# Attention of a two-layer encoder by pairs of heads: scores on the two halves of the array's rows, values on the two halves of its columns

## The chip, the cores and the metric

One core of one Trainium2 chip runs the kernel. The metric is the device time of one execution in microseconds (us), the median of the runs shown. The engines are TensorE (PE, with its weight loads PEld), VectorE (DVE), ScalarE (ACT), GpSimd (POOL) and SyncE (SP, which issues DMAs). Each engine works through its own instructions in a fixed order and waits at an instruction until what it needs is there.

## The reference

Two layers, 512 tokens, 1024 channels. Cut to what the change touches:

```
proj = h @ w_in[layer]                       # 2048 columns: pool | q | k | v
y_pool = pool_mixer(u_pool, ...)             # 4 groups of 128, trailing means over 2, 4, 8, 16
# stick-breaking attention, 8 heads of 64:
z = einsum('bhtd,bhsd->bhts', qb, kb) * scale
log_1m_beta = where(mask, log_sigmoid(-z), 0)
between = cumsum(log_1m_beta, axis=3, reverse=True) - log_1m_beta
att = where(mask, exp(log_sigmoid(z) + between), 0)
y_sb = einsum('bhts,bhsd->bhtd', att, vb)
mix = concat([y_pool, y_sb]) @ w_out[layer]
h = LayerNorm(alpha * h + mix);  h = LayerNorm(alpha * h + FFN(h))   # dense, then top-2-of-8 experts
```

## The kernel before

Numbers are kept as pairs of float16 (a high part and a rest), so each product is three matmuls: high by high, high by rest, rest by high. Each layer begins with a mixer, the part that the change touches; the dense layer and the experts after it are the same before and after.

In the mixer all is laid out with the source position on the partitions. A head's scores z stand in three banks of PSUM (pool `pz`, two tiles), 1280 columns: four blocks of 512, 384, 256 and 128 columns, since only later positions look at a block. `head_z` (L326) makes them from q and k: a head has 64 channels, so its 12 matmuls use 64 of the array's 128 rows, the lower half for an even head and the upper half for an odd one. Then, in two parts of 768 and 512 columns, ACT forms abs, exp and ln (L330 to L332), DVE adds max(z, 0) (L333), POOL masks the diagonal blocks (L344), and DVE splits the result into two float16 tiles (L346, L347). `head_att` adds the reverse running sum to z by matmuls with a triangle and with ones (L355, L360; 20 matmuls), ACT takes exp (L364), and POOL and DVE mask and split again. `head_out` (L379) multiplies by v: 12 matmuls on all 128 columns of the array for the 128 channels of a pair of heads, of which ACT copies the head's own 64 partitions into `cat` (L381).

The loop over heads issues, for each head `hd`: `head_att(hd)`, `head_out(hd - 1)`, one or two `pool_map`s if there are any, `head_z(hd + 2)`, and then a piece of other work of about 10 us on PE: the projection of a later pair's q and k (`qk_proj`), two groups of the pooling mixer (`pool`), v's second half (`v_proj`), the split of `cat`, or the output projection (`w_out`). `pool` makes u by 48 matmuls; `pool_group` copies it (ACT L284), forms the trailing sums on DVE (L290 to L298) and splits them (ACT L274 into `pdh`, DVE L276 into `pdl`); `pool_map` is three matmuls (L310 to L312) and a copy by ACT (L313). A scheduler puts the instructions of the whole program into one order per engine when the kernel is built; in the mixer that order follows the order in which the code issues the work, with small moves.

Three stores matter. `pa` has two PSUM tiles (tag `acc`), taken in turns by `qk_ps`, `u_ps`, `v_ps`, `o_ps`, `pool_ps` and `mix_ps`: a new one waits until the one before the last has been copied out. `pz` has two tiles, one for each of two heads. The weights of the mixer are split long before they are used (ACT L153, DVE L154); the rows of L153 and L154 that stand between the heads belong to the output projection.

Of the kernel before, what the change touches and what calls it, by code (L numbers as in the profile page):

```python
# [17 lines left out]
P = 128  # L18
D = 1024
# [44 lines left out]
class Trunk:  # L64
# [248 lines left out]
        nc.scalar.activation(cat[:, g, :], ps, AF.Copy, scale=sc[:, g:g + 1])  # L313


    def head_z(self, hd, qk):
        nc, mm = self.nc, self.nc.tensor.matmul
        (qh, ql), (kh, kl) = qk
        r = slice(hd % 2 * HD, (hd % 2 + 1) * HD)
        z = self.pz.tile([P, 1536], F32, tag="z", name="z")  # L320
        for i in (1, 3, 2, 0):
            T = S - i * P
            o = z[:, ZOFF[i]:ZOFF[i] + T]
            ks = slice(i * P, (i + 1) * P)
            for n, (kk, qq) in enumerate(((kh, qh), (kl, qh), (kh, ql))):
                mm(o, kk[r, ks], qq[r, i * P:], start=(n == 0 and i != 3), stop=False, skip_group_check=True)  # L326
        t = self.bp.tile([P, W], F32, tag="bf", name="t", bufs=3)
        s2 = self.head_pair()
        for c, blocks in HALVES:
            nc.scalar.activation(t[:, c], z[:, c], AF.Abs)  # L330
            nc.scalar.activation(t[:, c], t[:, c], AF.Exp, scale=-1.0)
            nc.scalar.activation(t[:, c], t[:, c], AF.Ln, bias=1.0)  # L332
            nc.vector.scalar_tensor_tensor(t[:, c], z[:, c], 0.0, t[:, c], op0=ALU.max, op1=ALU.add)  # L333
            self.head_two(t, s2, c, blocks)
        return z, t, s2

    def head_pair(self):
        return [self.bp.tile([P, W], F16, tag="br", name="sh", bufs=4) for _ in range(2)]

    def head_two(self, t, s2, c, blocks, scale=1.0):  # L340
        nc = self.nc
# [23 lines left out]
            self.head_two(t, a2, c, blocks, AS)  # L365
        return a2

    def head_out(self, hd, a2, v, cat):
        nc, mm = self.nc, self.nc.tensor.matmul
        vh, vl = v  # L370
        ah, al = a2
        p = hd // 2
        r = slice(hd % 2 * HD, (hd % 2 + 1) * HD)
        o = self.pa.tile([P, 512], F32, tag="acc", name="o_ps")
        c = slice(p % 2 * P, (p % 2 + 1) * P)
        for i in (1, 2, 3, 0):
            T = S - i * P
            for n, (vv, x) in enumerate(((vh, ah), (vh, al), (vl, ah))):
                mm(o[:, i * P:], vv[:, i, c], x[:, ZOFF[i]:ZOFF[i] + T], start=(i == 1 and n == 0),  # L379
                   stop=(i == 0 and n == 2), skip_group_check=True)  # L380
        nc.scalar.activation(cat[r, 4 + p, :], o[r, :], AF.Copy, scale=1.0 / (AS * VS))  # L381


    def mixer(self, l, h, hs, first=None):
# [24 lines left out]
        def qk_proj(p, ps=None):  # L409

            w = self.unit(win[2 + p])
            acc = [self.pa.tile([P, 512], F32, tag="acc", name="qk_ps") if ps is None else ps[:, 512 * s:512 * s + 512]
                   for s in range(2)]
            qk[p] = [tuple(mp.tile([P, S], F16, tag=f"qk{s}", name="qk", bufs=4) for _ in range(2)) for s in range(2)]
            for ts in (slice(0, S),) if ps is None else (slice(0, S // 2), slice(S // 2, S)):
                for s, sc in ((0, QS * XS), (1, KS * XS)):
                    self.chan_major(acc[s][:, ts], hs, w, s, ts)
                    if ts.stop == S:
                        self.two(*qk[p][s], acc[s], sc)
                    yield  # L420
# [18 lines left out]
        if first:  # L439
            with tc.issue_after(self.normed[1]), tc.issue_after(self.normed[2]):  # L440
                self.constants(self.cp, mp.tile([P, 16 + S], F32, tag="pf", name="room", bufs=2))
        zt, at = {}, {}
        zt[0] = self.head_z(0, qk[0])
        zt[1] = self.head_z(1, qk[0])
        list(qk_proj(1))
        ms = None
        wu = {}
# [19 lines left out]
        def cat_split(ks):  # L467
            for k in ks:
                self.two(ms[0][:, k], ms[1][:, k], cat[:, k, :].rearrange("p (t c) -> p t c", c=P))

        early = (4, 5, 0, 1, 2, 3)
        for hd in range(2 * NPAIR - 1):
            at[hd] = self.head_att(zt.pop(hd))
            if hd >= 1:
                self.head_out(hd - 1, at.pop(hd - 1), v, cat)
            for n in range(1 + (hd > 3)):
                if maps:
                    g, d2 = maps.pop(0)
                    self.pool_map(params, g, d2, cat)
            if hd + 2 < 2 * NPAIR:  # L480
                zt[hd + 2] = self.head_z(hd + 2, qk[(hd + 2) // 2])
            if hd == 0:
                list(qk_proj(2))
            elif hd == 1:
                pool(0)
            elif hd == 2:
                pool(1)
            elif hd == 3:
                list(qk_proj(3))
            elif hd == 4:  # L490
                list(v_proj(1))
                ms = self.act_tiles(self.hp, "k t")
                cat_split(early)
            elif hd == 5:
                for tt in range(NT):
                    w_out(0, early, tt)
        at[7] = self.head_att(zt.pop(7))
        cat_split((6,))
        for tt in range(NT):
            w_out(1, (*early, 6), tt)  # L500
        for hd in (6, 7):
            self.head_out(hd, at.pop(hd), v, cat)
        cat_split((7,))
        wu[2] = self.unit(a["w_out"][l, 2])
        ctx.close()
# [738 lines left out]
    def build(self, dump=None):  # L1244
        nc, tc, a = self.nc, self.tc, self.a
        with ExitStack() as ctx:
            self.ctx = ctx
            pool = lambda name, bufs, **k: ctx.enter_context(tc.tile_pool(name=name, bufs=bufs, **k))
            cp = self.cp = pool("const", 1)
            self.sp = pool("small", 2)  # L1250
            self.rps, self.n_raw, self.ahead = [pool("raw", RAW)], 0, []
            self.wp = pool("split", 6)
            self.chain, self.feed, self.fed, self.pending = None, None, False, []
            hpool = pool("h", 1)
            self.pa = pool("pa", 2, space=PSUM)
            dram = pool("dram", 1, space=DRAM)
            self.H = dram.tile([S, D], F32, name="H")
            self.H2 = dram.tile([S, D], F32, name="H2")
            self.Y = dram.tile([NOROW + 1, D], F32, name="Y")
            self.hctx = ExitStack()  # L1260
            self.hp = self.hctx.enter_context(tc.tile_pool(name="act", bufs=1))
            self.ident = cp.tile([P, P], F32, name="ident")
            make_identity(nc, self.ident)
            self.mhalf = cp.tile([P, 1], F32, name="mhalf")
            nc.vector.memset(self.mhalf, -0.5)
            h = hpool.tile([P, NT, D], F32, name="h")
            nc.sync.dma_start(h[:, 0, :], a["x"][0:P, :])
            hs = self.act_tiles(self.hp)
            self.todo = {}

            def first(mp):
                gt, bt = (mp.tile([P, W], F32, tag="bf", name=n, bufs=3)[:, :D] for n in ("gt", "bt"))
                keep = tc.keep_in_program_order
                keep(nc.sync.dma_start(gt, a["ln_in_g"].to_broadcast([P, D])))
                keep(nc.sync.dma_start(bt, a["ln_in_b"].to_broadcast([P, D])))

                def norm(tt):
                    if tt > 0:
                        keep(nc.sync.dma_start(h[:, tt, :], a["x"][tt * P:(tt + 1) * P, :]))
                    self.ln_tile(h[:, tt, :], h[:, tt, :], gt, bt)  # L1280

                def step(pool, tt):
                    if tt + 1 < NT:
                        norm(tt + 1)
                    self.transpose_tile(hs, h[:, tt, :], tt, pool)

                norm(0)
                self.todo = {tt: lambda pool, tt=tt: step(pool, tt) for tt in range(NT)}

            def show():  # L1290
                for tt in range(NT):
                    nc.sync.dma_start(a["out"][tt * P:(tt + 1) * P, :], h[:, tt, :])
                self.a2ctx.close()
                self.hctx.close()

            for l in range(DEPTH):
                hs = self.mixer(l, h, hs, None if l else first)
                if dump == f"mix{l}":
                    return show()
                if l == 0:  # L1300
                    hs = self.dense(h, hs, a["ln2_g"][l:l + 1], a["ln2_b"][l:l + 1])
                    if dump == "ffn0":
                        return show()
                    self.a2ctx.close()
                else:
                    self.moe(h, hs, a["out"], a["ln2_g"][l:l + 1], a["ln2_b"][l:l + 1])
# [56 lines left out]
```

## Time and profile before

| | |
|---|---|
| median of 3 runs | 1627.39 us (1625.93 to 1628.72) |
| profiled execution | 1625.76 us, its span 1624.0 us |
| PE busy | 94% of the span |
| DVE, ACT, POOL busy | 73%, 57%, 11% |
| mean granted clock of PE | 0.986 of 2.4 GHz |
| first layer's mixer, heads | about 50 to 180 us |
| second layer's mixer, heads | about 588 to 717 us |

A matmul's duration in the trace holds its way through the array, so that durations of matmuls that follow each other overlap; what one costs PE is read from start to start. The same holds, less so, on DVE and ACT: an instruction starts some 0.1 us before the one ahead ends if it doesn't need its result.

### The profile page before, as it was taken

The page shows a single profiled execution, that of the slowest core. Times are in us where ns is not written, and L with a number is a line of the kernel's source. Part 1 is how long each engine was busy: PE and PEld are TensorE (multiplying, and loading weights), DVE is VectorE, ACT ScalarE, POOL GpSimd, SP SyncE. Part 2 cuts the span into 40 slices and gives each one's busy share as a digit, 9 for nine tenths or more (in the row PEclk, how much of TensorE's full clock was granted, in tenths as well). Part 3 has the DMA queues.
Part 4 walks back from the last instruction along what each step waited for, and adds up shares of the span by engine and source line. Part 5 has one row for each costly group of instructions (what it writes and reads, how often), then busy time and mean ns, then how long its engine had stood idle before and what let it go on. Part 6 is the DMA issues. An engine that isn't in the chain of part 4 may idle for free.

```text
span 1624.0 us, 41584 instructions
## 1 busy us (share of the span) xinstructions
PE 1530.3 (94%) x17978; PEld 1277.5 (79%) x17978; DVE 1184.5 (73%) x1682; ACT 929.8 (57%) x1276; POOL 178.1 (11%) x297
## 2 busy tenths in 40 slices
PE   6999999999999999998999999995999999999975
PEld 4547774674755865686999999995999999999975
DVE  8786673333433767758998988876788799898986
ACT  5656243222223355624587877764677678777861
POOL 4122110000000212212000001000000000000423
PEclk9999999999999999999999999997999999999997
DMA  8410153222322132024899999898699869999992
GB/s 301 173 53 27 53 207 104 98 78 101 110 89 94 62 130 78 27 103 158 319 344 388 377 383 360 308 338 284 231 383 335 317 243 418 414 393 356 340 367 88
DMA packets 61840, 366.75 MB, mean 226 GB/s; under 512 B 9654, under 2 KB 13582, under 8 KB 28628
## 3 DMA queue, kind: packets, MB, share of 16 engines
q1 hardware_dynamic: 55044, 351.65, 58.1%
q0 software_dynamic: 5312, 9.21, 2.4%
q10 hardware_dynamic: 1296, 3.18, 0.6%
q8 instruction: 142, 2.33, 0.6%
q14 instruction: 46, 0.38, 0.1%
HBM read 353.17 MB, written 10.84 MB: 224 GB/s over the span
## 4 chain that ended last, share of the span: by engine, by line
PE 51%; issue 26%; DVE 7%; DMA 6%; ACT 3%; POOL 3%; POOLq 0%; SPq 0%; ACTq 0%; DVEq 0%
PE gu L1158 24%; PE acc L1158 14%; DVE wl L154 3%; DMA xr<-H,idx 3%; PE z L326 1%; DMA raw<-in_moe_wd 1%; PE qk_ps L267 1%; PE qk_ps L268 1%; PE qk_ps L269 1%; POOL rs L220 1%; ACT wh L153 1%; DMA h<-Y,r_rows 1%; PE yt_ps L1213 1%; DMA H<-h 1%; PE z L360 1%
## 5 line engine op out<-in xcount | busy, mean ns | idle before, releaser
L154 DVE SCALAR_TENSOR_TENSOR wl<-raw,wh 128x512 f16<-128x512 f32 (+2 forms) x506 | 754.3, 1516 | 59.0 <-ACT wh L153 55.7
L153 ACT ACTIVATE wh<-raw 128x512 f16<-128x512 f32 (+2 forms) x506 | 631.1, 1274 | 264.3 <-PE gu L268 90.5
L1158 PEld LDWEIGHTS <-wh 128*128 128x128 f16 x8448 | 668.0, 97 | 3.1 <-DVE xT L1153 2.3
L1158 PE MATMUL gu<-xT,wh 128*128 128x128 f16 (+6 forms) x5632 | 522.9, 224 | 2.2 <-DVE xT L1153 2.2
L1158 PE MATMUL gu<-xT,wl 128*128 128x128 f16 (+6 forms) x2816 | 517.8, 223 | 0.0
L1158 PEld LDWEIGHTS <-wl 128*128 128x128 f16 x4224 | 416.6, 99 | 3.2 <-issue 3.1
L1158 PE MATMUL acc<-hT,wh 128*128 128x128 f16 (+6 forms) x2816 | 261.9, 225 | 3.1 <-DVE hT L1180 2.9
L1158 PE MATMUL acc<-hT,wl 128*128 128x128 f16 (+6 forms) x1408 | 259.4, 223 | 0.0
L268 PE MATMUL gu<-hTl,wh 128*128 128x512 f16 (+1 forms) x384 | 138.7, 361 | 0.5 <-DVE hTl L276 0.5
L267 PE MATMUL gu<-hTh,wh 128*128 128x512 f16 (+1 forms) x384 | 138.7, 361 | 0.0
L269 PE MATMUL gu<-hTh,wl 128*128 128x512 f16 (+1 forms) x384 | 138.7, 361 | 0.0
L588 DVE SCALAR_TENSOR_TENSOR sg<-gu,sg 128x512 f32<-128x512 f32 (+1 forms) x24 | 15.5, 646 | 138.7 <-PE gu L269 138.7
L267 PEld LDWEIGHTS <-wh 128*128 128x128 f16 x608 | 59.5, 98 | 61.6 <-issue 3.1
L269 PEld LDWEIGHTS <-wl 128*128 128x128 f16 x608 | 59.5, 98 | 59.2 <-issue 1.3
L268 PEld LDWEIGHTS <-wh 128*128 128x128 f16 x608 | 59.5, 98 | 58.3 <-issue 2.5
L1175 ACT ACTIVATE sg<-gu 128x128 f32<-128x128 f32 (+6 forms) x176 | 49.7, 283 | 89.1 <-PE gu L1158 85.7
L611 PE MATMUL d_ps<-wh,tl 128*128 128x256 f16 x352 | 96.0, 273 | 0.1
L611 PE MATMUL d_ps<-wh,th 128*128 128x256 f16 x352 | 95.9, 273 | 0.0
L611 PE MATMUL d_ps<-wl,th 128*128 128x256 f16 x352 | 95.9, 273 | 0.0
L1128 POOL DMA_INDIRECT xr<-H,idx x12 | 22.6, 1883 | 627.3 <-DMA raw<-in_moe_gu 399.5
L344 POOL TENSOR_SCALAR_AFFINE_SELECT t<-t 128x128 f32<-128x128 f32 x128 | 58.7, 486 | 185.9 <-DVE t L333 131.8
L1179 ACT ACTIVATE hT<-hu 128x128 f16<-128x128 f32 (+6 forms) x176 | 55.5, 315 | 36.3 <-DVE hu L1177 33.9
(226 smaller groups left out, 1933.7 us busy)
## 6 DMA issues: line engine op xcount, KB each, us to landing
raw<-in_moe_gu SPq DMA_DIRECT2D x176, 1024.0 KB
raw<-in_moe_wd SPq DMA_DIRECT2D x64, 896.0 KB
raw<-in_moe_wd SPq DMA_DIRECT2D x32, 1024.0 KB
raw<-in_ffn_gu SPq DMA_DIRECT2D x22, 1024.0 KB
raw<-in_w_in SPq DMA_DIRECT2D x16, 1024.0 KB
raw<-in_w_out SPq DMA_DIRECT2D x8, 1024.0 KB
raw<-in_ffn_wd SPq DMA_DIRECT2D x8, 896.0 KB
raw<-in_ffn_wd SPq DMA_DIRECT2D x4, 1024.0 KB
```

The costliest lines, as they stand in the source:

```text
L153: self.link(lambda: self.nc.scalar.activation(wh[:, c], raw[:, c], AF.Copy, scale=WS))
L154: self.link(lambda: self.nc.vector.scalar_tensor_tensor(wl[:, c], raw[:, c], WS, wh[:, c], op0=ALU.mult, op1=ALU.subtract))
L220: nc.gpsimd.tensor_tensor(rs, ve, self.mhalf, op=ALU.pow)
L267: mm(ps, wh[:, k, :], hh[:, k, ts], start=(k == 0), stop=False)
L268: mm(ps, wh[:, k, :], hl[:, k, ts], start=False, stop=False)
L269: mm(ps, wl[:, k, :], hh[:, k, ts], start=False, stop=(k == KD - 1))
L344: nc.gpsimd.affine_select(out=b, in_=b, pattern=[[1, P]], base=0, channel_multiplier=-1, compare_op=ALU.is_gt, fill=0.0)
L611: nc.tensor.matmul(ps[:, :256], hid[f][x][:, ts], v[:, f - f0, :], start=(f == f0 and n == 0), stop=(f == f1 - 1 and n == 2))
L1128: nc.gpsimd.indirect_dma_start(out=xr[b], out_offset=None, in_=self.H, in_offset=bass.IndirectOffsetOnAxis(ap=idx[b], axis=0), bounds_chec ...
L1158: self.nc.tensor.matmul(o, w, x[:, a], start=(start and n == 0), stop=(stop and n == 2), skip_group_check=True)
L1175: self.link(lambda: nc.scalar.activation(sg, ps[:, :N], AF.Silu, scale=XS))
L1179: self.link(lambda: nc.scalar.activation(hT[:, 0, :], hu, AF.Copy))
```

## The change

`head_z` becomes `pair_z`: both heads of a pair, with their matmuls in turns (even head, odd head), each on its half of the rows. `head_out` becomes `pair_out`: each head multiplies by its own 64 columns of v, in turns, into its own 64 partitions of one `o_ps`, and one copy by ACT (L385) takes all 128 partitions. The loop goes over pairs: attention of both heads, then the other work, then the next pair's scores, this pair's values, and behind them the pool maps and the next projection. Buffers: `t` 4 for 3, the split tiles 6 for 4.

```
-    def head_z(self, hd, qk):
+    def pair_z(self, qk):
...
             for n, (kk, qq) in enumerate(((kh, qh), (kl, qh), (kh, ql))):
-                mm(o, kk[r, ks], qq[r, i * P:], start=(n == 0 and i != 3), stop=False, skip_group_check=True)
+                for s, z in enumerate(zs):
+                    r = slice(s * HD, (s + 1) * HD)
+                    mm(z[:, ZOFF[i]:ZOFF[i] + T], kk[r, ks], qq[r, i * P:], start=(n == 0 and i != 3), stop=False,
+                       skip_group_check=True)
...
-    def head_out(self, hd, a2, v, cat):
+    def pair_out(self, p, a2s, v, cat):
...
-                mm(o[:, i * P:], vv[:, i, c], x[:, ZOFF[i]:ZOFF[i] + T], start=(i == 1 and n == 0),
-                   stop=(i == 0 and n == 2), skip_group_check=True)
-        nc.scalar.activation(cat[r, 4 + p, :], o[r, :], AF.Copy, scale=1.0 / (AS * VS))
+                for s, a2 in enumerate(a2s):
+                    c = slice(p % 2 * P + s * HD, p % 2 * P + (s + 1) * HD)
+                    mm(o[s * HD:(s + 1) * HD, i * P:], vv[:, i, c], a2[a][:, ZOFF[i]:ZOFF[i] + T],
+                       start=(i == 1 and n == 0), stop=(i == 0 and n == 2), skip_group_check=True)
+        nc.scalar.activation(cat[:, 4 + p, :], o, AF.Copy, scale=1.0 / (AS * VS))
...
+        for p in range(NPAIR):
+            at = [self.head_att(x) for x in zt]
+            if p < 2:
+                pool(p)
+            elif p == 2:
+                pool_maps()
+                list(v_proj(1))
+            else:
+                cat_split((6,))
+                for tt in range(NT):
+                    w_out(1, (*early, 6), tt)
+            if p + 1 < NPAIR:
+                zt = self.pair_z(qk[p + 1])
+            self.pair_out(p, at, v, cat)
+            if p < 2:
+                pool_maps()
+                list(qk_proj(2 + p))
+            elif p == 2:
+                ms = self.act_tiles(self.hp, "k t")
+                cat_split(early)
                 for tt in range(NT):
                     w_out(0, early, tt)
```

On PE, behind the first half of the pooling mixer in the first layer, before: the values of head 1, one pool map, then the scores of head 4 (z_1047).

```order
L379 MATMUL o_ps_1028<-sh_847,vl_196 128x512
L310 LDWEIGHTS pw_h_468
L310 MATMUL pool_ps_1042<-pdh_951,pw_h_468 128x512
L311 LDWEIGHTS pw_h_468
L311 MATMUL pool_ps_1042<-pdl_952,pw_h_468 128x512
L312 LDWEIGHTS pw_l_469
L312 MATMUL pool_ps_1042<-pdh_951,pw_l_469 128x512
L326 LDWEIGHTS qk_773
L326 MATMUL z_1047<-qk_771,qk_773 128x384
```

On PE at the same place in the changed kernel: the last values of the pair (sh_713 is head 0's, sh_745 head 1's), both pool maps (pool_ps_938, pool_ps_943), and the next projection.

```order
L383 MATMUL o_ps_912<-sh_713,vl_196 64x512
L383 LDWEIGHTS vl_196
L383 MATMUL o_ps_912<-sh_745,vl_196 64x512
L310 LDWEIGHTS pw_h_468
L310 MATMUL pool_ps_938<-pdh_803,pw_h_468 128x512
...
L310 LDWEIGHTS pw_h_468
L310 MATMUL pool_ps_943<-pdh_844,pw_h_468 128x512
...
L267 LDWEIGHTS wh_950
L267 MATMUL qk_ps_960<-hTh_90,wh_950 128x512
```

Two `pool_ps` and a `qk_ps` now follow `o_ps` directly, all in the two tiles of `pa`; before, one map stood there and the scores, which have tiles of their own, came next.

On ACT, from the copy of the second group's u onward, before: the copy of `o_ps` (L381) stands two rows ahead of the first part of the next head's abs (L330), and `pdh` of the second group behind that.

```order
L284 ACTIVATE cat_119<-u_ps_955 128x512
L153 ACTIVATE wh_1945<-raw_1943 128x512 x3
L364 ACTIVATE t_738<-z_725 128x768
L364 ACTIVATE t_738<-z_725 128x512
L381 ACTIVATE cat_119<-o_ps_1028 64x512
L313 ACTIVATE cat_119<-pool_ps_1042,pw_s_472 128x512
L330 ACTIVATE t_1060<-z_1047 128x768
L274 ACTIVATE pdh_992<-pd_988 128x512
```

On ACT at the same place in the changed kernel (t_874 and t_893 are the two heads of the next pair, pdh_844 the second group's).

```order
L284 ACTIVATE cat_119<-u_ps_807 128x512
L153 ACTIVATE wh_1805<-raw_1803 128x512 x3
L334 ACTIVATE t_874<-z_848 128x768
L334 ACTIVATE t_893<-z_849 128x768
L335 ACTIVATE t_874<-t_874 128x768
L274 ACTIVATE pdh_844<-pd_840 128x512
L336 ACTIVATE t_874<-t_874 128x768
L335 ACTIVATE t_893<-t_893 128x768
L385 ACTIVATE cat_119<-o_ps_912 128x512
L334 ACTIVATE t_874<-z_848 128x512
L336 ACTIVATE t_893<-t_893 128x768
L335 ACTIVATE t_874<-t_874 128x512
```

The copy of `o_ps` has moved behind the `pdh` of the second group and behind five rows of the next pair; the copy of the first map (L313) is the row after the last one shown.

## Rows read from the trace of the kernel before

**Rows 1.** The page, busy time, share of the span and instructions of each engine.

```profile
PE 1530.3 (94%) x17978; PEld 1277.5 (79%) x17978; DVE 1184.5 (73%) x1682; ACT 929.8 (57%) x1276; POOL 178.1 (11%) x297
```

**Rows 2.** Windows in both mixers: stretch, length, busy time (instructions) by engine, granted clock, DMA.

```profile
61.00:97.00 36.00, 34.51 (x205) 18.16 (x205) 27.19 (x49) 23.45 (x39) 8.19 (x22) 1.00 0.16 59
97.00:134.00 37.00, 36.14 (x208) 18.35 (x206) 29.74 (x55) 23.13 (x38) 12.36 (x27) 1.00 0.17 57
...
636.00:672.00 36.00, 35.60 (x205) 18.19 (x205) 29.15 (x54) 22.67 (x38) 11.44 (x25) 1.00 0.18 59
```

**Rows 3.** Timeline of PE, rows with idle time: start, us, instructions, [idle before <-releaser].

```profile
61.42 0.49 PE L355 MATMUL z<-sh,ntri 128*128 128x128 f16 x4 [0.46 <-DVE t L333]
...
63.96 0.38 PE L355 MATMUL z<-sh,ntri 128*128 128x512 f16 x1 [1.07 <-DVE sh L347]
...
115.18 1.79 PE L326 MATMUL z<-qk 64*128 64x384 f16 x12 [0.86 <-ACT t L364]
...
149.73 1.79 PE L326 MATMUL z<-qk 64*128 64x384 f16 x12 [0.30 <-ACT t L364]
```

**Rows 4.** Timeline of PE around the scores of one head.

```profile
66.12 0.38 PE L267 MATMUL qk_ps<-hTh,wh 128*128 128x512 f16 x1
66.44 1.80 PE L326 MATMUL z<-qk 64*128 64x384 f16 x12
68.17 0.39 PE L268 MATMUL qk_ps<-hTl,wh 128*128 128x512 f16 x1
```

**Rows 5.** Timeline of PE at heads 0 and 1, whose scores follow each other.

```profile
51.63 2.53 PE L326 MATMUL z<-qk 64*128 64x384 f16 x23
54.09 0.39 PE L269 MATMUL qk_ps<-hTh,wl 128*128 128x512 f16 x1
```

**Rows 6.** Timeline of PEld in 52.2 to 52.6, the same place.

```profile
52.13 0.49 PEld L326 LDWEIGHTS <-qk 64*128 64x128 f16 x7
```

**Rows 7.** Timeline of PE from a head's values to the pool map behind them.

```profile
95.22 0.49 PE L379 MATMUL o_ps<-sh,vh 128*128 128x384 f16 x2
...
96.85 0.38 PE L310 MATMUL pool_ps<-pdh,pw_h 128*128 128x512 f16 x1
97.07 0.38 PE L311 MATMUL pool_ps<-pdl,pw_h 128*128 128x512 f16 x1
```

**Rows 8.** Timeline of ACT after the last matmul of a pooling half.

```profile
93.02 0.63 ACT L153 ACTIVATE wh<-raw 128x512 f16<-128x512 f32 x1 [1.35 <-PE u_ps L268]
93.56 0.58 ACT L284 ACTIVATE cat<-u_ps 128x512 f32<-128x512 f32 x1
94.04 1.65 ACT L153 ACTIVATE wh<-raw 128x512 f16<-128x512 f32 x3
```

**Rows 9.** Timeline of DVE right behind it.

```profile
94.30 0.15 DVE L290 COPY ps<-cat 128x1 f32<-128x1 f32 x1
...
94.96 0.68 DVE L154 SCALAR_TENSOR_TENSOR wl<-raw,wh 128x512 f16<-128x512 f32 x1
95.56 0.68 DVE L293 TENSOR_TENSOR ps<-ps 128x512 f32<-128x512 f32 x1
```

**Rows 10.** Groups of ACT by shape in 48 to 215: count | busy us, mean ns | idle before.

```profile
L331 ACT ACTIVATE t<-t 128x768 f32<-128x768 f32 x8 | 6.7, 840 | 0.2
...
L381 ACT ACTIVATE cat<-o_ps 64x512 f32<-64x512 f32 x8 | 4.7, 590 | 12.0 <-PE o_ps L379 12.0
...
L313 ACT ACTIVATE cat<-pool_ps,pw_s 128x512 f32<-128x512 f32 x4 | 2.7, 685 | 0.5 <-PE pool_ps L312 0.3
L274 ACT ACTIVATE pdh<-pd 128x512 f16<-128x512 f32 x4 | 2.5, 629 | 8.2 <-DVE pd L298 8.2
```

**Rows 11.** Timeline of PE in the experts, behind its idle time at 792 to 795.

```profile
794.90 0.19 PE L1042 MATMUL sl_ps<-terms,hot 128*128 128x6 bf16 x2 [3.05 <-DVE terms L1027]
```

**Rows 12.** Windows of PE alone: stretch, length, busy (instructions), granted clock, DMA.

```profile
796.20:799.50 3.30, 3.30 (x38) 0.50 0.99 353
1139.00:1144.30 5.30, 5.30 (x49) 0.50 0.01 3
```

More of the change, by code (lines that the diff above doesn't have):

```diff
@@ L313, in pool_map @@
         nc.scalar.activation(cat[:, g, :], ps, AF.Copy, scale=sc[:, g:g + 1])
-    def head_z(self, hd, qk):
+    def pair_z(self, qk):
         nc, mm = self.nc, self.nc.tensor.matmul
         (qh, ql), (kh, kl) = qk
-        r = slice(hd % 2 * HD, (hd % 2 + 1) * HD)
-        z = self.pz.tile([P, 1536], F32, tag="z", name="z")
+        zs = [self.pz.tile([P, 1536], F32, tag="z", name="z") for _ in range(2)]
         for i in (1, 3, 2, 0):
             T = S - i * P
-            o = z[:, ZOFF[i]:ZOFF[i] + T]
             ks = slice(i * P, (i + 1) * P)
             for n, (kk, qq) in enumerate(((kh, qh), (kl, qh), (kh, ql))):
-                mm(o, kk[r, ks], qq[r, i * P:], start=(n == 0 and i != 3), stop=False, skip_group_check=True)
[L327 to L335, printed above, removed]
+                for s, z in enumerate(zs):
+                    r = slice(s * HD, (s + 1) * HD)
+                    mm(z[:, ZOFF[i]:ZOFF[i] + T], kk[r, ks], qq[r, i * P:], start=(n == 0 and i != 3), stop=False,
+                       skip_group_check=True)
+        pair = []
+        for z in zs:
+            t = self.bp.tile([P, W], F32, tag="bf", name="t", bufs=4)
+            s2 = self.head_pair()
+            for c, blocks in HALVES:
+                nc.scalar.activation(t[:, c], z[:, c], AF.Abs)
+                nc.scalar.activation(t[:, c], t[:, c], AF.Exp, scale=-1.0)
+                nc.scalar.activation(t[:, c], t[:, c], AF.Ln, bias=1.0)
+                nc.vector.scalar_tensor_tensor(t[:, c], z[:, c], 0.0, t[:, c], op0=ALU.max, op1=ALU.add)
+                self.head_two(t, s2, c, blocks)
+            pair.append((z, t, s2))
+        return pair
     def head_pair(self):
-        return [self.bp.tile([P, W], F16, tag="br", name="sh", bufs=4) for _ in range(2)]
+        return [self.bp.tile([P, W], F16, tag="br", name="sh", bufs=6) for _ in range(2)]
     def head_two(self, t, s2, c, blocks, scale=1.0):
@@ L366, in head_att @@
         return a2
-    def head_out(self, hd, a2, v, cat):
+    def pair_out(self, p, a2s, v, cat):
         nc, mm = self.nc, self.nc.tensor.matmul
         vh, vl = v
-        ah, al = a2
-        p = hd // 2
-        r = slice(hd % 2 * HD, (hd % 2 + 1) * HD)
         o = self.pa.tile([P, 512], F32, tag="acc", name="o_ps")
-        c = slice(p % 2 * P, (p % 2 + 1) * P)
         for i in (1, 2, 3, 0):
             T = S - i * P
-            for n, (vv, x) in enumerate(((vh, ah), (vh, al), (vl, ah))):
-                mm(o[:, i * P:], vv[:, i, c], x[:, ZOFF[i]:ZOFF[i] + T], start=(i == 1 and n == 0),
-                   stop=(i == 0 and n == 2), skip_group_check=True)
-        nc.scalar.activation(cat[r, 4 + p, :], o[r, :], AF.Copy, scale=1.0 / (AS * VS))
+            for n, (vv, a) in enumerate(((vh, 0), (vh, 1), (vl, 0))):
+                for s, a2 in enumerate(a2s):
[3 more added lines that the diff above has]
+        nc.scalar.activation(cat[:, 4 + p, :], o, AF.Copy, scale=1.0 / (AS * VS))
     def mixer(self, l, h, hs, first=None):
@@ L441, in mixer @@
                 self.constants(self.cp, mp.tile([P, 16 + S], F32, tag="pf", name="room", bufs=2))
-        zt, at = {}, {}
-        zt[0] = self.head_z(0, qk[0])
-        zt[1] = self.head_z(1, qk[0])
+        zt = self.pair_z(qk[0])
         list(qk_proj(1))
@@ L469, in cat_split, with pool_maps @@
                 self.two(ms[0][:, k], ms[1][:, k], cat[:, k, :].rearrange("p (t c) -> p t c", c=P))
+        def pool_maps():
+            while maps:
+                g, d2 = maps.pop(0)
+                self.pool_map(params, g, d2, cat)
         early = (4, 5, 0, 1, 2, 3)
[L472 to L490, printed above, removed]
-                list(v_proj(1))
+        for p in range(NPAIR):
[4 more added lines that the diff above has]
+                pool_maps()
+                list(v_proj(1))
+            else:
[9 more added lines that the diff above has]
+            elif p == 2:
                 ms = self.act_tiles(self.hp, "k t")
                 cat_split(early)
-            elif hd == 5:
                 for tt in range(NT):
                     w_out(0, early, tt)
[L497 to L502, printed above, removed]
         cat_split((7,))
@@ L1271, in first @@
             def first(mp):
-                gt, bt = (mp.tile([P, W], F32, tag="bf", name=n, bufs=3)[:, :D] for n in ("gt", "bt"))
+                gt, bt = (mp.tile([P, W], F32, tag="bf", name=n, bufs=4)[:, :D] for n in ("gt", "bt"))
                 keep = tc.keep_in_program_order
```

## The prediction, made before the result was known

> **What bounds the kernel now.** I read the page's busy line first: PE is busy 94% of the span, DVE 73%, ACT 57% [rows 1]. An average over many stages does not say what bounds the two mixers, so next come the windows laid over their heads: PE works 34.5 of 36 us and 36.1 of 37 in the first layer, 35.6 of 36 in the second, at the full clock, while DVE and ACT have room of 7 to 9 and 13 to 14 us [rows 2]. Then the timeline of PE over the first layer's heads, its rows with idle time: four, 0.46 + 1.07 + 0.86 + 0.30 = 2.7 us, the first two while the very first attention waits for DVE [rows 3]. So PE is the bound of the mixers, and a microsecond of PE saved there counts, as long as nothing that PE waits for becomes later than PE.
>
> **What the change saves on PE (one layer; the second runs the same code).** Scores first. A lone head's 12 matmuls cost 0.10 to begin (66.12 to 66.44 is 0.32, where a matmul of 512 columns has a pace of 0.22, [rows 7]) and 1.73 to the next `qk_ps` [rows 4], 1.83 together, 3.66 a pair. If two halves of the rows work beside each other, a pair costs what one head does now. The trace bears that out in part: heads 0 and 1, issued one after the other, take 51.63 to 54.09 = 2.46 us for 23 recorded matmuls [rows 5], a good microsecond less than 2 x 1.73. I take 1.83 a pair, with 3.66 as the other end (nothing overlaps): three pairs save 3 x 1.83 = 5.5, pair 0, which overlaps already, only about 0.7.
>
> Values. Twelve matmuls on all columns take 95.22 to 96.85 = 1.63 us a head [rows 7], 3.26 a pair. No row of before works on halves of columns, so the price is bounded: 1.83 if they run as scores do (half, and 0.2 to switch), 3.46 if nothing overlaps and the switching is added. In between lies the case that the 24 weight loads, twice as many instructions for the same columns, set the pace: loads of half the rows come every (0.49 - 0.09) / 6 = 0.07 us [rows 6], 24 of them 1.6, which is no bound. I take 1.83, nearest to the rows of the scores: 4 x 1.43 = 5.7. Together 5.5 + 0.7 + 5.7 = 11.9 us a layer, 23.8 in both. Four copies of `o_ps` a layer go too (590 ns each on ACT, [rows 10]); ACT has room, so they are worth nothing by themselves.
>
> The Trainium skill, in "TensorEngine Tiling (Array Packing)", section "Restrictions", says that tiling by columns takes away the fast form of the weight load. Our rows show loads on half of the rows only, so they can't tell; if slower loads could no longer hide behind the matmuls, the values would come out at the far end, 3.46 a pair, which is the price that rival C below has from the rows.
>
> **What the change makes wait.** The new order puts the values, both pool maps and the next projection directly behind each other, and all take their tile from `pa`, which has two. So the second map waits for the copy of `o_ps` (L385), the projection for the copy of the first map (L313); behind the waiting map stands everything on PE, since an engine doesn't go past a wait. Before, one map stood there, and scores, with tiles of their own, followed. On ACT L385 stands behind `pdh` of the second pooling group and behind rows of the next pair's scores, so it ends late. I follow the chain from the end of the last `u_ps` matmul.
>
> Pair 0. ACT ends one L153 and copies u; DVE's L290 starts 94.30 - 93.02 = 1.28 later [rows 8, 9]. On DVE L290 to the next full row takes 0.66, then five full rows at a pace of 0.60 (94.96 to 95.56, [rows 9]), because rows of L154 (weight splits for later) stand between the trailing sums as they do now, and two short ones: 4.2, the short ones estimated at a quarter of a microsecond each. `pdh` 0.63 [rows 10] and the hand-over 0.1: 6.2. Then, ahead of L385, two ACT rows of 768 columns at 0.84 less the 0.10 that neighbours overlap, 1.48, and L385 itself 0.59 [rows 10]: 8.25. PE meanwhile has the next scores 1.83, the values 1.83 and the first map 3 x 0.22 = 0.66 [rows 7], 4.3. The second map waits **3.9**. Then the projection waits for L313, four rows behind L385 (0.5 + 0.74 + 0.5 for the parts of 512, 768 and 512 columns, and 0.69, [rows 10]) = 2.4, less the second map's 0.66: **1.75**. 5.65 in all.
>
> Pair 1. The same chain, with the group of window 16, whose sums have two full rows more, 1.2: 9.5 against 4.3, a wait of **5.2**, and about 0.45 for the projection. 5.65 again.
>
> Pair 2. The second `mix_ps` waits for L385, which here stands behind six splits of `cat` (0.53 each, by L274 less its overlap, 3.2), one of v and two each of three scores' rows (0.74 x 6): about 8.5 from the end of v. PE has scores 1.83, values 1.83 and the first `mix_ps`, 18 matmuls of 256 columns at half of 0.22, 2.0: wait **3.0**; and since the scores began late on ACT, head 6's attention waits another 0.9.
>
> Pair 0's start keeps DVE as its limit; with both heads' attention one behind the other it waits some 0.9. Sum of waits: 5.65 + 5.65 + 3.9 + 0.9 = 16.1 a layer against 2.7 before, so 13.4 more against 11.9 less: +1.5 a layer. A second way of adding, the mixer followed row by row at these paces, gave +2.3. I take +1.5, +3 for both, where every term of the chain is good to perhaps 1 us in each stage, so ±5 for both layers. What the shorter values save is mostly hidden here: at pairs 0 to 2 PE arrives at the wait earlier and waits longer.
>
> The Trainium skill's same page says, under "PSUM Bottleneck", that packing the array makes TensorE faster but not the emptying of PSUM, so that the copy may become the limit. That is the kind of wait I compute from the rows, and it speaks against the change; the trace agrees with it only so far as the copy's 590 ns a tile and the room in `pa` allow, for the wait is made by ACT's order more than by the copy's length.
>
> **The clock.** Idle time has a second price. After PE stood idle for 3.05 us in the experts [rows 11] its granted clock was 0.50, that is 1.2 GHz, for the stretch of 3.3 us read there [rows 12]: a loss of half of it, 1.65. Waits of up to 1.07 in the mixers were followed by none, the clock there being 1.00 [rows 2, 3]. The waits of 3.9 and 5.2 are longer than the one that was followed by a fall, the 3.0 of pair 2 about as long. I take one fall for each of the first two, 2 x 1.7 a layer, 6.8 in both; the bounds are nothing and, by the longer stretch of 5.3 us at 0.50 [rows 12], 2.65 for each of three, 16.
>
> **Sum.** Profiled execution 1625.8 (span 1624.0 and 1.8 around it) + 3 + 6.8 = 1635.6. The median of the runs shown lies 1.6 above that execution: **1637**.
>
> DVE and POOL have the same rows as before in another order, and each SP transfer of the mixer's weights lands long before its use, so neither adds a term; the buffers of `t` and of the split tiles (4 and 6) let the two heads of the next pair begin while this pair's values still read theirs.
>
> **Rivals.**
> A, the forecast: waits of 3.9 and 5.2 with a clock fall behind each, 1637; 0.38.
> B, the same waits without a fall: 1637 - 6.8 = 1630; with the ±5 it reaches below 1627. For it: nothing in the mixers fell so far. Against: those waits were a third as long. 0.27.
> C, the change doesn't do what it says on columns: halves of the columns don't overlap. Of 4 x 1.63 a layer all but the last pair's meet a wait that shrinks by as much, so 2 to 3 a layer is lost: 1641 to 1643. For it: no row shows them side by side. Against: rows do so [rows 5]. 0.07.
> D, the side of faster: the copy of `o_ps` comes sooner than I have it, because ACT, with room of 13 us in 36 [rows 2], is ahead of my chain, and PE doesn't reach the second map before. Without any new wait the gain is whole, 1627 - 24 = 1603; with half of the 13.4 a layer, 1627 - 24 + 13 = 1616, with no fall of the clock. It decides in favour of faster as soon as the waits stay under some 12 us a layer. Against it: L385 can't pass `pdh`, which needs the whole of the sums. 0.18.
> E, the chain is longer: DVE, which in these stages also splits the attention's results, delays the sums by 2 us a stage. Six stages make 12 more: 1649. For it: DVE is at 30 of 37 us [rows 2]. 0.10.
>
> **Chances.** A measurement of this kernel tells about 0.2%, 3.25 us, from no change, so the edges are 1624 and 1630.6. Faster: D, less its top end, and a little of B: 0.20. Within: half of B and a little of D and A: 0.18. Slower: the rest, 0.62. The range reaches from D's half gain to E: 1614 to 1650; A's own is 1630 to 1645.
>
> **What would show it.** In the profile after: the scores of a pair take some 1.8 us from the matmul ahead to the one behind, and so do the values; 3.3 for the values would be C. PE's idle time before L310 of the second map is 3.9 and 5.2 us, released by ACT's L385; before the next `qk_ps` 1.75 and 0.45, released by L313; before the second `mix_ps` 3.0. The granted clock of 0.50 shows behind the two long waits in both layers; full clock there is B. The forecast is wrong in its core if PE's idle time in a mixer stays under 10 us, and in its sign if PE's time of all mixers' rows falls by more than the idle time grows.

## The result and the profile after

The changed kernel takes 1638.84 us (median of 4 runs, 1637.96 to 1640.34) against 1627.29 (4 runs, 1625.93 to 1628.72): ratio 1.0072, interval 1.0054 to 1.0089. It is slower by 11.6 us. Run again later beside others it took 1641.73 against 1628.35, ratio 1.0080 (1.0068 to 1.0092).

The page's busy line [rows 1] now reads:

```profile
PE 1521.5 (93%) x17978; PEld 1268.3 (78%) x17978; DVE 1185.2 (72%) x1682; ACT 918.6 (56%) x1268; POOL 172.4 (11%) x297
```

PE has as many instructions, and its busy time fell by only 8.8 us, less than the 23.8 that the change was to save: part of the busy time is now at half the clock. Next the windows laid over each mixer, from its first scores to the first transposes behind it, first of before, then of after (columns: stretch, length, busy time and instructions of PE, PEld, DVE, ACT and POOL, granted clock, DMA):

```profile
50.61:194.60 143.99, 139.78 (x982) 89.61 (x982) 98.88 (x175) 82.88 (x138) 32.03 (x75) 1.00 0.15 52
589.11:732.64 143.53, 140.21 (x984) 89.71 (x984) 98.93 (x175) 78.60 (x130) 32.07 (x75) 1.00 0.20 72
```

```profile
49.90:200.90 151.00, 134.74 (x981) 83.87 (x981) 99.60 (x175) 77.33 (x134) 29.24 (x75) 0.94 0.15 50
595.41:745.57 150.16, 135.01 (x983) 84.68 (x984) 99.60 (x175) 73.05 (x126) 29.25 (x75) 0.94 0.19 69
```

The mixers grew by 7.0 and 6.6 us, 13.6 together; the stretch between them is 394.51 in both. Everything outside the mixers took 1.4 less in this execution, which is chance (the last experiment). So the whole loss lies in the mixers. Where it lies is told by the rows of PE with idle time, first layer, in answer to [rows 3] (timeline of PE):

```profile
63.41 0.38 PE L360 MATMUL z<-sh,ntri 128*128 128x512 f16 x1 [0.43 <-DVE sh L352]
83.91 0.58 PE L310 MATMUL pool_ps<-pdh,pw_h 128*128 128x512 f16 x1 [4.51 <-ACT cat L385]
86.22 0.58 PE L267 MATMUL qk_ps<-hTh,wh 128*128 128x512 f16 x1 [0.88 <-ACT cat L313]
123.48 0.59 PE L310 MATMUL pool_ps<-pdh,pw_h 128*128 128x512 f16 x1 [5.07 <-ACT cat L385]
...
161.00 0.27 PE L256 MATMUL mix_ps<-wh,hTh 128*128 128x256 f16 x1 [2.72 <-ACT cat L385]
...
178.27 0.27 PE L256 MATMUL mix_ps<-wh,hTh 128*128 128x256 f16 x1 [1.10 <-DVE h L458]
```

Idle time in the mixer, its length less PE's busy time and without the 0.8 us just ahead of the transposes, is 15.5 us against 3.4 before; in the second layer 14.4 against 2.5. Both maps' waits are released by L385, the copy of `o_ps`.

The price of scores and values, in answer to [rows 4, 7], from the timeline of PE ahead of the first of these waits:

```profile
75.09 1.80 PE L327 MATMUL z<-qk 64*128 64x384 f16 x24
76.82 0.52 PE L383 MATMUL o_ps<-sh,vh 128*64 128x384 f16 x4
...
78.58 0.39 PE L310 MATMUL pool_ps<-pdh,pw_h 128*128 128x512 f16 x1
```

24 matmuls of scores take 76.82 - 75.09 = 1.73, as many as 12 did; 24 of values 78.58 - 76.82 = 1.76. Both halves work side by side. The weight loads for half of the columns do not set the pace, though each is a little longer (groups of PEld in the first mixer: 109 ns, where the loads of all columns take 98):

```profile
L383 PEld LDWEIGHTS <-vh 128*64 128x64 f16 x64 | 3.0, 109 | 1.9 <-issue 0.6 <-DVE pdl L276 0.4 <-ACT hTh L274 0.4
```

Why L385 is late is seen on ACT over the same stretch, with its answer to [rows 8]:

```profile
78.44 1.50 ACT L334 ACTIVATE t<-z 128x768 f32<-128x768 f32 x2
79.82 0.85 ACT L335 ACTIVATE t<-t 128x768 f32<-128x768 f32 x1
81.28 0.63 ACT L274 ACTIVATE pdh<-pd 128x512 f16<-128x512 f32 x1 [0.61 <-DVE pd L298]
81.81 0.83 ACT L336 ACTIVATE t<-t 128x768 f32<-128x768 f32 x1
82.55 0.83 ACT L335 ACTIVATE t<-t 128x768 f32<-128x768 f32 x1
83.28 0.58 ACT L385 ACTIVATE cat<-o_ps 128x512 f32<-128x512 f32 x1
```

`o_ps` was complete at about 78.8; its copy stands behind `pdh`, which waits for DVE's sums, and two rows of scores, and starts at 83.28. The other part of the map's need, on DVE:

```profile
81.08 0.16 DVE L298 TENSOR_TENSOR pd<-pd,cat 128x3 f32<-128x3 f32 x1
81.94 0.69 DVE L276 TENSOR_TENSOR pdl<-pd,pdh 128x512 f16<-128x512 f32 x1 [0.69 <-ACT pdh L274]
```

The second map's own input `pdl` was finished at 82.6, only 1.2 us ahead of L385's end.

Last the clock, windows of PE alone in answer to [rows 12]: stretch, length, busy, granted clock, DMA.

```profile
86.00:88.00 2.00, 1.78 (x5) 0.50 0.00 0
88.00:91.40 3.40, 3.40 (x10) 0.50 0.00 0
91.40:95.00 3.60, 3.60 (x18) 0.96 0.02 5
...
123.40:129.20 5.80, 5.72 (x14) 0.50 0.01 4
...
161.00:163.00 2.00, 2.00 (x19) 1.00 0.00 0
...
705.00:708.00 3.00, 2.84 (x18) 0.68 0.02 5
```

Behind the wait of 4.51 us PE works at 0.50, 1.2 GHz, until 91.7, behind that of 5.07 until 129.2. Busy time times the missing share of the clock, added over windows of 2.5 us, is the loss: 6.3 us in the first mixer (3.5 and 2.9 behind the two long waits), 6.9 in the second (3.7, 1.5, and 1.7 behind the third wait). Behind the 2.72 us of the third wait the clock stays full in the first layer and falls in the second.

The balance: the mixers are longer by 7.0 and 6.6, idle time grew by 12.1 and 11.8, the clock took 6.3 and 6.9; so PE's own work fell by 12.1 + 6.3 - 7.0 = 11.4 and 11.8 + 6.9 - 6.6 = 12.1 us. The idle time alone just about eats the saving; the loss over before is what the clock takes.

### The profile page after: what moved, and what is told of

Same layout as the page of the kernel before. It is cut to its first block, busy times and chain, and to the rows that moved or that the text cites. A ratio compares the mean times of both kernels' runs of the same rounds, so it can differ in the third digit from the quotient of the medians.

```text
span 1636.2 us, 41552 instructions
## 1 busy us (share of the span) xinstructions
PE 1521.5 (93%) x17978; PEld 1268.3 (78%) x17978; DVE 1185.2 (72%) x1682; ACT 918.6 (56%) x1268; POOL 172.4 (11%) x297
## 4 chain that ended last, share of the span: by engine, by line
PE 49%; issue 26%; DVE 8%; DMA 6%; ACT 4%; POOL 3%; POOLq 0%; ACTq 0%; DVEq 0%; SPq 0%
PE gu L1156 24%; PE acc L1156 14%; DVE wl L154 3%; DMA xr<-H,idx 3%; PE qk_ps L267 1%; DMA raw<-in_moe_wd 1%; PE qk_ps L268 1%; PE qk_ps L269 1%; POOL t L349 1%; POOL rs L220 1%; PE z L365 1%; DMA h<-Y,r_rows 1%; PE z L360 1%; PE yt_ps L1211 1%; DMA H<-h 1%
## 5 line engine op out<-in xcount | busy, mean ns | idle before, releaser
L586 DVE SCALAR_TENSOR_TENSOR sg<-gu,sg 128x512 f32<-128x512 f32 (+1 forms) x24 | 15.5, 645 | 138.7 <-PE gu L269 138.7
L256 PE MATMUL mix_ps<-wh,hTh 128*128 128x256 f16 x256 | 70.6, 276 | 7.8 <-ACT cat L385 5.4
```

The costliest lines, as they stand in the source:

```text
L256: mm(ps, hh[:, k, tt], wh[:, k, :], start=(k == ks[0] and not part), stop=False)
```

## The experiments

"Mixers" are the two stretches of the windows above. Idle time and clock loss of a mixer are worked out as above.

**Pool maps behind the projection, maps_late.**

```
-                pool_maps()
                 list(qk_proj(2 + p))
+                pool_maps()
```

> The changed kernel, with the two pool maps of a pooling half issued behind the next projection instead of ahead of it; nothing else. Theory (the saving on PE is whole, and it is lost to the two tiles of the accumulator, whose copies stand late in ACT's order, and to the clock falls behind these waits): the copy of the values ends at about 83.9 us in the first layer, by then PE has worked off the first half of the projection, so the waits of 4.5, 0.9 and 5.1 us become about 1 us each half, and with them the stretches at 0.50 behind them (3.2 us each) go: 8.5 + 6.4 = 15 us a layer, 1609 us. Rival (PE merely runs ahead of ACT and DVE, whose work is the same; a wait removed here comes back at the next attention, which needs the next scores split): the waits come back there with some 4 us a half, without falls of the clock: 1622 to 1626.

Measured 1619.68, ratio 0.9952 (0.9937 to 0.9966): moving one line turns a loss into a gain over before. Mixers 140.6 and 140.5, 10.4 and 9.7 less than the change. Idle time fell by 7.1 and 6.4 and the clock's loss from 6.3 and 6.9 to 3.3 and 3.4. The mechanism is borne out, but two thirds of the gain came, not all: the maps themselves now wait, for the projection's copies out of the same two tiles, and the clock fell behind the first of these waits and behind that of the output projection, which stayed.

```profile
93.36 0.38 PE L310 MATMUL pool_ps<-pdh,pw_h 128*128 128x512 f16 x1 [2.25 <-DVE qk L278]
```

The rival's wait at the next attention did not come: there PE waits for nothing.

**The splits of `cat` earlier as well, maps_late_split_early.** `cat_split(early)` moves from behind the third pair's values to ahead of `v_proj(1)`.

> As maps_late, and the six splits of the concatenated tile are issued ahead of v's second half instead of behind the third pair's values, so that on ACT the copy of these values no longer stands behind them. Theory: the wait of 2.7 us before the second tile of the output projection goes as well, 5 to 6 us less than maps_late, 1604. Rival (the splits only move: ahead of v's second half they delay the splits of the third pair's attention on DVE by 6 x 0.6 us, and the values wait for these): no better than maps_late, or up to 3 us worse.

1618.38, ratio 0.9944 (0.9923 to 0.9965); mixers 140.2 and 140.0, 0.4 and 0.5 less than maps_late. The wait of 2.72 fell to 0.64, but the values now wait 0.80 and 0.90 for v's split, which stands behind the moved splits on ACT and DVE. The rival was right.

**Values ahead of the scores, values_first.** `self.pair_out(p, at, v, cat)` moves ahead of `zt = self.pair_z(qk[p + 1])`.

> The changed kernel, with the values of a pair issued ahead of the next pair's scores; nothing else. It puts the copy of the values on ACT ahead of the second pooling group's split and of all rows of the next scores. If the tile that the values hold is the whole cause, the waits of 4.5 and 5.1 us all but go: 1627 or less. Theory (the copy is only the last of a row of things that come late): the second map needs its own input, whose low part DVE finishes at 82.6 us against 83.9 for the copy, so 3.1 to 3.3 of the 4.5 stay; and ACT now stands idle ahead of the split until the sums are there, so that the scores' rows and behind them the copy of the first map come later, up to 87 us, and the projection waits about 3 us more instead of 0.9. Both falls of the clock stay. 1639 to 1645.

1643.26, ratio 1.0100 (1.0076 to 1.0123). Mixers 151.1 and 151.5. Here L385 ran at 78.93, long before the second map, and yet the waits stayed (PE):

```profile
82.44 0.59 PE L310 MATMUL pool_ps<-pdh,pw_h 128*128 128x512 f16 x1 [2.56 <-ACT pdh L274]
...
87.35 0.58 PE L267 MATMUL qk_ps<-hTh,wh 128*128 128x512 f16 x1 [3.17 <-ACT cat L313]
```

ACT of the same kernel shows the second one's cause: it stands idle ahead of `pdh`, and six rows of scores follow it.

```profile
81.76 0.63 ACT L274 ACTIVATE pdh<-pd 128x512 f16<-128x512 f32 x1 [2.25 <-DVE pd L298]
82.30 1.49 ACT L334 ACTIVATE t<-z 128x768 f32<-128x768 f32 x2
...
86.61 0.68 ACT L313 ACTIVATE cat<-pool_ps,pw_s 128x512 f32<-128x512 f32 x1
```

So the tile was the last of several late things. What has to move is the map, not the copy.

**Values by pairs alone, in the old order of heads, values_by_pairs_only.** The split tiles have 8 buffers, and

```
-            if hd >= 1:
-                self.head_out(hd - 1, at.pop(hd - 1), v, cat)
+            if hd in (2, 4, 6):
+                self.pair_out(hd // 2 - 1, [at.pop(hd - 2), at.pop(hd - 1)], v, cat)
```

> The kernel before with its order of heads and its scores, and with only the values changed: both heads of a pair in turns on the halves of the columns, behind the attention of the next pair's first head (the split tiles have 8 buffers instead of 4). Theory (halves of the columns work side by side, 1.76 us a pair as in the profile of the changed kernel against 3.26): 4 x 1.5 a layer, 12 in both, 1615 us if nothing waits anew. Rival (the values' time is hidden by other waits of these stages, or the later copy makes the next map wait): 1624 to 1630.

1619.12, ratio 0.9947 (0.9933 to 0.9962). Mixers 140.8 and 140.9, 3.2 and 2.7 less than before. PE's work fell by 5.4 in each (3.2 + 0.5 idle + 1.7 clock; 2.7 + 1.0 + 1.7), near the 6.0 expected, and the time lies between the two that were expected; with the values gone from that place PE reaches head 5's scores before their tile is free:

```profile
114.81 1.79 PE L326 MATMUL z<-qk 64*128 64x384 f16 x12 [1.72 <-ACT t L364]
```

and its window, with the clock in it:

```profile
115.00:121.00 6.00, 6.00 (x25) 0.72 0.08 11
```

**Head 5's scores later, values_by_pairs_z5_late.** `next(steps)` of `qk_proj(3)` is issued ahead of them, the rest behind.

> As values_by_pairs_only (old order of heads, values by pairs), with the scores of head 5 issued between the two halves of the last projection instead of ahead of it. There PE waited 1.72 us for ACT's exp of head 3 to leave its PSUM tile, and lost 1.7 to the clock behind it, in each layer. Theory: both go, 2 x 3.4 less than 1619.1, 1612. Rival (the scores come 5 us later, and head 5's attention waits for their split): part of it comes back there, 1615 to 1619.

1617.09, ratio 0.9936 (0.9919 to 0.9952); mixers 138.95 and 138.90, 1.9 and 2.0 less. No fall of the clock is left in either, which is worth the 1.7 a mixer; the wait only changed its place: 0.76, 0.42 and 0.17 us now stand at 130 to 132, two of them for copies out of the two tiles. Of the 6.8 expected the mixers gained 3.9; the time, 2.0 us lower than that of values_by_pairs_only, lies in the rival's range.

**Turns taken out, turns_off_both** (on maps_late): the loop over the two heads goes outside the loops over blocks, in `pair_z` and `pair_out`.

> maps_late with the turns taken out: the scores of both heads, and the values of both heads, issued one head after the other, on the same halves of the array. If the array pairs them by itself in whatever order, scores and values of a pair stay at 1.73 and 1.76 us. If only neighbours in the queue work side by side, the scores take 2.46 as heads 0 and 1 did in the kernel before, and the values between 2.4 and 3.3. In time that is 0.7 x 4 and 0.6 to 1.5 x 4 a layer at most, 10 to 18 us in both, of which the waits before the maps and before the output projection hide a part: 1625 to 1635 against 1619.7.

```profile
77.95 2.69 PE L327 MATMUL z<-qk 64*128 64x384 f16 x24
80.57 0.51 PE L383 MATMUL o_ps<-sh,vh 128*64 128x384 f16 x2
...
83.28 0.39 PE L267 MATMUL qk_ps<-hTh,wh 128*128 128x512 f16 x1
```

Scores 2.62, values 2.71. Two lone heads' scores would be 2 x 1.73 = 3.46, so about half of the gain comes with one head right behind the other, the rest with the turns. Where the heads meet, the second head's first matmul (384 columns) starts at 78.84, ahead of the first head's last three (512 columns), which stand before it in the queue and start at 78.94, 79.16 and 79.37. From two narrow windows of PE; a row merges several matmuls and has the start and the shape of its first one:

```profile
78.84 0.71 PE L327 MATMUL z<-qk 64*128 64x384 f16 x6
...
79.16 0.62 PE L327 MATMUL z<-qk 64*128 64x512 f16 x7
```

Without turns a pair costs 0.89 + 0.95 more, 7.4 us of PE work a layer. The time, though, is 1621.71, ratio 0.9962 (0.9951 to 0.9974), near maps_late's; its mixers are 140.8 and 141.2, only 0.2 and 0.7 longer. Idle time fell by 4.1 and 3.7, and the clock's loss of 3.3 and 3.4 is gone entirely. With waits behind it, PE's saving is paid back twice, as idle time and as clock. I had expected the waits to hide a part; they hid nearly all.

**Maps put off to the next pair, maps_between and maps_between_split_half.** One map goes behind each head's attention; the second kernel also issues four of the six splits ahead of `v_proj(1)`.

```
-            at = [self.head_att(x) for x in zt]
+            at = []
+            for x in zt:
+                at.append(self.head_att(x))
+                if maps:
+                    g, d2 = maps.pop(0)
+                    self.pool_map(params, g, d2, cat)
```

> The changed kernel with the pool maps of a half put off to the next pair, one behind each head's attention there, and with four of the six splits of the concatenated tile ahead of v's second half, two behind the third pair's values. maps_late still had waits of 2.25 and 1.24 us before its maps (for the projection's own copies), 0.5 before the projection and 2.7 before the second tile of the output projection, and lost 6.3 us to the clock behind them in both layers. Theory (each wait is a matter of what stands in the two tiles): the two waits before the maps go, the one of 2.7 becomes about 1.2, and with them most of the clock's loss: 2 x 5 + 5 = 15 less than maps_late's 1619.7, 1605. Rival (PE is now at the pace of ACT and DVE): the time goes to new waits at the attention, and it stays at 1615 to 1620.

> The one half of maps_between_split_half: the pool maps of a half put off to the next pair, one behind each head's attention, and the splits of the concatenated tile left where the change has them. Theory: as maps_late without its waits of 2.25 and 1.24 us before the maps and what the clock lost behind them, but with the wait of 2.7 before the second tile of the output projection and a fall of about 1.4 behind it in each layer: 1608.5 + 2 x (2.7 - 1.8 + 1.4) - 2 x 0.7 for the wait of 0.7 that the half split had brought = 1612. Rival (the early half of the splits did it): 1616 to 1619.

1608.51, ratio 0.9888 (0.9872 to 0.9905), with both; 1611.16, ratio 0.9897 (0.9880 to 0.9913), with the maps alone. Both beat the kernel before by about 1%. The windows of the mixers in maps_between:

```profile
52.11:186.68 134.57, 129.21 (x981) 83.18 (x982) 98.98 (x175) 77.36 (x134) 28.64 (x75) 0.99 0.16 55
581.21:715.83 134.62, 129.28 (x984) 83.33 (x984) 99.08 (x175) 73.20 (x126) 28.55 (x75) 0.99 0.21 77
```

With the same instructions on PE as in the change each mixer is 16 us shorter. Idle time is 4.5; the 2.73 before the output projection stays, with a clock loss of 1.4 to 1.5 behind it. The half split makes that wait 1.84, with no fall of the clock behind it, but brings 0.69 before the values; its mixers, 134.3 and 134.4, gain 0.2 to 0.3. The maps did it. The expected times were 3.5 too low with both and 0.8 too high with the maps alone.

**The long waits filled with useless work, first_map_seven_times.**

```
+        for _ in range(1 if g % 2 else 7):
```

ahead of the three matmuls of `pool_map`.

> The changed kernel with useless work in its two long waits: the three matmuls of the first map of each half are issued seven times instead of once, 6 x 0.65 = 3.9 us more work for PE at a place where it stood idle for 4.5 and 5.1 us; the last round gives the result. On ACT the copy of that map moves back by one row in the first half and by four in the second, so that the projection behind it waits some 0.5 and 1.5 us more, 4 in both layers. Theory (half of the loss is the clock, that falls behind the waits): no fall of the clock any more, 13 us less lost, so in spite of more work it is faster than the changed kernel: 1638.8 - 13 + 4 = 1630. Rival (only the idle time counts, and the rows at 0.50 are no loss of their own since PE waits for ACT and DVE anyway): 1639 to 1643.

1641.17, ratio 1.0088 (1.0071 to 1.0105): by the time, the rival's number. The profile's mixers say another thing (windows as above):

```profile
53.11:202.48 149.37, 138.00 (x1017) 86.28 (x1018) 99.62 (x175) 77.53 (x134) 28.61 (x75) 0.99 0.15 50
597.01:744.88 147.87, 137.59 (x1019) 86.80 (x1019) 99.59 (x175) 73.28 (x126) 28.64 (x75) 0.99 0.19 70
```

149.4 and 147.9 us, 3.9 less than the change with 15.6 us more work. The waits before the maps shrank to 0.63 and 1.19 in the first layer, those before the projection grew to 2.17 and 1.60, so that idle time fell by only 4.9 in each mixer, and the clock lost 1.4 to 1.5 in place of 6.3 and 6.9. With 7.8 us more work for 4.9 less idle time a mixer would be 2.9 longer if the clock took as much as before; it is 1.6 and 2.3 shorter. What lies outside the mixers was 6.9 us longer than in the change's profile. Three kernels were therefore measured once more on one chip.

> The changed kernel once more, beside first_map_seven_again on the same chip. In the profiles so far the two mixers, from the first scores to the first transposes behind them, took 151.0 and 150.2 us in the changed kernel and 149.4 and 147.9 with the first map seven times; but what lies outside them, the same instructions, took 6.9 us longer there. Theory (what lies outside differs from one execution to the next and has nothing to do with the edit): the mixers are again 151.0 and 150.2 to within 0.3, and the time stands at 1637 to 1640.

> first_map_seven_times once more. Theory (outside by chance): the mixers again 149.4 and 147.9, the outside as in change_again, and the time 2 to 5 us below change_again's. Rival (the longer outside belongs to this kernel): the outside is again some 7 us longer than in change_again, and the time 1 to 3 us above it.

> maps_between once more. Its mixers took 134.6 us each against 134.3 and 134.4 in maps_between_split_half, which stood 2.7 us lower in time; outside the mixers its profile has 3.5 us more. Theory (by chance): the mixers 134.6 again and the time 1608 to 1611, no worse than maps_between_split_half by more than 1. Rival (it belongs to the kernel): 1611 to 1612 again.

| kernel | time, ratio to before | mixers | outside them |
|---|---|---|---|
| change_again | 1641.73, 1.0080 (1.0068 to 1.0092) | 150.5, 150.0 | 1336.8 |
| first_map_seven_again | 1640.72, 1.0074 (1.0061 to 1.0087) | 147.9, 149.1 | 1337.4 |
| maps_between_again | 1609.59, 0.9887 (0.9873 to 0.9902) | 134.8, 134.9 | 1337.4 |

The change itself came out 1.7 us above its expected range, its first mixer 0.5 shorter, not within 0.3. The mixers repeat to 0.2 to 1.5 us, and the useless work shortens them again, by 3.5 in all; what lies outside varies between 1335 and 1342 from one profile to the next and belongs to no kernel. So the clock's price is shown in the mixers, where 15.6 us of useless work cost less than nothing; in the whole time the gain of 1.0 lies within the intervals. I had expected 2 to 5 and 9: the longer wait before the projection took back more than I gave it.

## Why the prediction was right

Forecast 1637, measured 1638.84 (1641.73 when measured again), by rival A's mechanism; the nearness is partly luck, two errors that offset each other.

- **PE's saving.** 11.9 us a layer foretold, 11.4 and 12.1 worked out from the balance. The value taken for column halves, 1.83, was 1.76; rival C (3.46) fell. The Trainium skill says that column tiling disables the fast weight load ("TensorEngine Tiling (Array Packing)", section "Restrictions"); the trace shows 109 ns a load against 98, and the loads stay hidden.
- **The waits.** Foretold 3.9, 1.75, 5.2, 0.45 and 3.0; measured 4.51, 0.88, 5.07, none and 2.72, with the releasers that were named (L385, L313, L385, and L385). In the second layer the first three are 4.20, 0.88 and 4.76. All of a mixer, 16.1 against 15.5 and 14.4; the growth 13.4 against 12.1 and 11.8. Some of that nearness is chance too: pair 0's start waited 0.43 and head 6's attention some 0.5 in the first layer, not 0.9 each, while the 1.10 before the last part of the output projection (0.56 before) was not foretold. Rivals D (waits under 12 us) and E (2 us more a stage) fell.
- **Their cause.** I put the wait down to the copy standing late in ACT's order. That is the releaser, but values_first shows that without it 2.56 of the 4.51 stay, since the map's own input is late. The term's size was right, its reading half right. The Trainium skill's "PSUM Bottleneck" on the same page is borne out in kind, a copy out of PSUM ends the wait, but the copy's 588 ns are not what made it late.
- **The clock.** The fall came behind both long waits, as taken, and the term was mis-sized: 1.7 a fall from the 3.3 us of [rows 12], where three of the four cost 2.9 to 3.7 and one 1.5, with a fifth of 1.7 at pair 2. In the first layer the stretches at 0.50 went on for 7.8 and 5.8 us, longer than the 5.3 of that group, so that the bound of 2.65 was passed too. Foretold 6.8 in both layers, lost 13.2.
- **The sum.** +3 and +6.8 foretold. Measured in the mixers: 12.1 + 11.8 of waits less 11.4 + 12.1 of savings, 0.4, and 13.2 for the clock, 13.6; less the 1.4 outside. The net of idle time and saving was 2.6 too high and the clock 6.4 too low. Rival B, waits without a fall, would have been no change: the sign hung on the clock, whose term was taken at half of what it came to.

That the waits and not the pairing made it slower is shown by maps_between: the same PE instructions, 1.1% faster than before.

## What to carry to other kernels

When an edit shortens the bounding engine's work, follow what it reaches earlier: here 11 to 12 us a layer saved became 12 us of waiting at two PSUM tiles, and the cure was to place a product whose input is late behind work that needs neither tile nor input. Count a long idle of PE twice, as idle time and as what the clock takes behind it. And read a small edit's effect in its own stretch of the profile: the stretch repeats to about a microsecond, the whole time here only to several.

## What had not been expected of the hardware

Matmuls on two halves of the array work side by side when they stand near each other in the queue: 1.73 and 1.76 us a pair in turns, 2.62 and 2.71 one head behind the other, where the second head's first matmul started ahead of the first head's last three. The stretches at 1.2 GHz behind waits of 4.2 to 5.1 us cost 1.4 to 3.7 us each. And waits of like length are followed by a fall or not: 1.72 us in values_by_pairs_only was, as were 2.25 in maps_late and 2.73 in maps_between; 2.72 in the first layer of the change and 1.84 in maps_between_split_half were not. The kernel's order alone does not decide it: the wait of 2.17 in first_map_seven_times was followed by a fall, the same wait in first_map_seven_again was not, and there one of 1.60 in the second layer was. What decides it in that range stays open.
